# Delta-net chunk inversion by squaring 8x8 blocks on TensorE, decays loaded in rows, scalings on ScalarE

## The chip, the core and the metric

The kernel runs on one core of one Trainium2 chip. Five engines work side by side, each through its own queue in program order: TensorE (PE, matrix products into PSUM), VectorE (DVE), ScalarE (ACT), GpSimd (POOL) and SyncE (SP, which here only issues DMAs). The metric is the device time of one execution in microseconds (us), as the median of several runs.

## The reference

One layer of a hybrid model over 256 latent and 256 context tokens of width 2048: a modulated norm, one input projection, two token mixers side by side (RWKV-7 with 16 heads of 64, gated DeltaNet with 8 heads of 128, both in two directions), a gated merge, an output projection, then a SwiGLU feed-forward. The change touches the DeltaNet mixer:

```python
gc = jnp.cumsum(chunks(g), axis=-1)                      # 64 tokens in a chunk
diff = gc[..., :, None] - gc[..., None, :]
decay = jnp.where(incl, jnp.exp(jnp.where(incl, diff, 0.0)), 0.0)
kb = kc * bc[..., None]
lmat = jnp.where(strict, jnp.einsum('nbhik,nbhjk->nbhij', kb, kc) * decay, 0.0)
rhs = jnp.concatenate([vc * bc[..., None], kb * jnp.exp(gc)[..., None]], axis=-1)
sol = lax.linalg.triangular_solve(lmat, rhs, left_side=True, lower=True, unit_diagonal=True)
```

So for each head, direction and chunk a unit triangular 64x64 matrix has to be inverted, from `lmat`, and `lmat` needs the decays between any two tokens, exp of a difference of running sums.

## The kernel before

Everything is fp32. Large projections are split into a high and a low part (`whi`, `wlo`) and done as three fast matmuls for each 128x128 weight tile; small products are plain fp32 matmuls, which the trace shows as two instructions each (a row of order says x8 where the profile says x16).

The program has four stretches. First the norm, the modulation and some low-rank projections (lines 404 to 522). Then the two mixers, woven together (lines 707 to 1481): the RWKV pairs `prepare`, `grams`, `inverse`, `values`, `scan` for p in 0..7, and the DeltaNet heads `features`, `tokens`, `decays`, `head_grams`, `head_inverse`, `head_scan` for h in 0..7. Then the merge and output projection (1485 to 1538), then the feed-forward (1541 to 1602).

In the woven stretch the pieces are Python generators. `Weave` (line 169) runs them against a table of costs and emits, on each engine, whichever instruction could start first by that table, with ranks for ties. This fixes the order on PE, DVE, ACT and POOL; at run time each queue goes through it strictly in that order. Filler for PE is `products` (line 1041), the projections of all heads with the lowest rank: 48 matmuls for each gate column block (256 columns) or for q, and 48 of 512 columns for k and v. The tables `GATES_A` and `GATES_B` (line 28) say behind which RWKV pair or DeltaNet head a gate block may be emitted: of the DeltaNet ones, 2 behind the grams of head 5, 6 behind those of head 6 and 8 behind those of head 7. `ada_rest` (line 1423) runs beside the DeltaNet heads: 96 tiles of a modulation weight, each with one DMA from POOL's queue and two DVE instructions (`aw`).

`invert` (line 552) does both mixers' inverses. It writes the matrices to DRAM (`scr`), reads the 16x16 diagonal blocks back one to a partition (`arena<-scr`), inverts them by substitution in 30 small DVE instructions (lines 583 to 588), writes them to DRAM (`tscr`), and reads them back in matrix layout (`T<-tscr`, `Tx<-tscr`). Two rounds on PE then double the blocks to 32 and to 64 (`double` in the change; lines 613 to 657 here). `head_inverse` (1317) joins two 64-blocks to 128 and writes `TF`. `decays` (1259) makes the decay matrix `Ed` of a head: DVE multiplies a mask by the gates (`arena<-C,gtok`), PE sums it (`pa<-arena,C`, 512 columns), ACT takes exp, POOL masks; a second matmul of 256 columns gives the row factor for `Qe`. `tokens` (1234) scales the transposed keys into `keg` and `kta`; `head_scan` (1351) goes through the four chunks, with `Vn` scaled by the gate `btok`.

PSUM is handed out as banks: `pib` one bank (inverses), `pab` two (everything else of a head), `psb` two (scans), `mmb` three (projections).

Of the kernel before, what the change touches and what calls it, by code (L numbers as in the profile page):

```python
# [18 lines left out]
P = 128  # L19
# [35 lines left out]
def const_array():  # L55
    c = np.zeros((P, NC_COLS), np.float32)

    def put(name, a):
        lo, hi = _C[name]
        c[:, lo:hi] = np.asarray(a, np.float32).reshape(P, hi - lo)  # L60

    i = np.arange(P)
    put("ident", np.eye(P))
    put("ones", np.ones((P, P)))
    put("bd64", (i[:, None] // 64) == (i[None] // 64))
    s, t = (i % 64)[:, None], np.arange(64)[None]
# [4 lines left out]
    put("qmask", np.concatenate([(same & (rb % 2 == 1))[:, even], (same & (rb % 2 == 0))[:, ~even]], 1))  # L71
    u = i[:, None]
    v = i[None]
    put("tri", np.concatenate([u <= v, u >= v], 1))
    put("aft", np.concatenate([u > v, u < v], 1))
# [192 lines left out]
def emit(ctx: ExitStack, tc, A, out, dbg=None):  # L268
# [34 lines left out]
    qmask = c_("qmask").rearrange("p (d a c) -> p d a c", d=2, a=2)  # L303
    tri = c_("tri").rearrange("p (d t) -> p d t", d=2)
    aft = c_("aft").rearrange("p (d t) -> p d t", d=2)
# [23 lines left out]
    zero = cst.tile([P, 130], F32, name="zero")  # L329
    G.memset(zero, 0.0)  # L330
# [74 lines left out]
    with tc.tile_pool(name="p0", bufs=1) as p0, \  # L405
# [95 lines left out]
        for part in range(NE + 1):  # L501
            if part < NE:
                ps = pst(pmm, "mm")
            for c in range(4):
                if part + 1 < NE:
                    load_ada(part + 1, c)
                if part < NE:
                    ada_part(ps, part, c)
                if c == 0 and part < NE:
                    w = low_split(part)  # L510
                    if part + 1 < NE:
                        load_low(part + 1)
                for _ in itertools.islice(before or (), (0, 1, 2, 1)[c]):
                    pass
            if part < NE:
                rows_of(part, ps, before or ())
                before = low_products(part, w)
            else:
                for _ in before:
                    pass  # L520
        for t in tscr:
            Q.dma_start(t.rearrange("(p a n) -> p a n", p=P, a=8), zero.unsqueeze(1).to_broadcast([P, 8, 130]))
# [29 lines left out]
    def invert(pool, Lt, parts, nu, which, full, fill):  # L552

# [42 lines left out]
        yield v.transpose(T0[:, us[1]], Tx[:, us[1]])  # L596

# [6 lines left out]

        def half(t, d):
            ax = "p u"[:2 * len(t.shape) - 3]
            return t.rearrange(f"{ax} (a b c) -> {ax} a b c", a=2, b=2)[..., d, :]

        def mm(ps, d, lhs, rhs):
            return [e.matmul(ps[64 * h:64 * h + 64, 32 * i:32 * i + 32], lhs(h, h2 * d + i), rhs(h, h2 * d + i),  # L610
                             start=True, stop=True) for i in range(h2) for h in range(2)]

        Qm = xt[:, :32 * nu].rearrange("p (u c) -> p u c", c=32)
        for d in range(2):
            T0d = half(T0[:, us[d]], d)
            ps = yield pib
            yield mm(ps, d, Lt, lambda h, u: half(N_(h, u), d))
            pv = ps[:, 0:32 * h2].rearrange("p (i a c) -> p i a c", a=2, c=16)
            yield v.tensor_mul(Qm[:, us[d]].rearrange("p i (a c) -> p i a c", a=2), pv,
                               qmask[:, d].unsqueeze(1).to_broadcast([P, h2, 2, 16]))  # L620
            yield mm(ps, d, Nt_, lambda h, u: Qm[64 * h:64 * h + 64, u, :])
            yield v.tensor_add(T0d, pv, T0d)
            weave.release(pib)
            yield v.transpose(Tx[:, us[d]], T0[:, us[d]])
# [19 lines left out]
        qo = pool.tile([P, h2, 32], F32, tag="ivo", name="qo")  # L644
# [6 lines left out]
        if full:  # L651
# [3 lines left out]
            for h in range(2):  # L655
# [8 lines left out]
    abd = dpool.tile([4, 32, P], F32, name="abd")  # L664
    gtok = cst.tile([P, 4, 16], F32, name="gtok")
# [12 lines left out]
               ("ivo", 256, 1), ("iv0", 1024, 1), ("v", 512, 1), ("gt", T, 1))  # L678
# [362 lines left out]
    def products():  # L1041
# [24 lines left out]
        while todo or nxt:  # L1066
# [27 lines left out]
            else:  # L1094
# [5 lines left out]
    gplaces = (("kvq", 1280, 2), ("l2s", 512, 1), ("gm", 512, 1), ("Ed0", 512, 1), ("Ed1", 512, 1), ("eq", T, 1), ("ob", 8 * T, 1),  # L1100
               ("NW", 1024, 1), ("O", T, 1), ("gy2", T, 1), ("q3", T, 1), ("XT", 512, 1), ("prod", 64, 1))
    shared = dict(kta=("LAl0", 1024, 3), LTg=("LAl1", 1024, 3), keg=("ivx", 1024, 2), iv0=("LAc0", 512, 3), ivx=("LAc0", 512, 3),
                  vt=("LAc1", 512, 3), PT0=("LAc1", 512, 3), PT1=("Pm", 512, 3), Qe=("Pm", 512, 3), Vn=("bon", T, 3), ivo=("bon", T, 3),
# [24 lines left out]
    gs = Shared()  # L1128
    hd = [{} for _ in range(NGH)]
# [6 lines left out]
    def begin():  # L1136
# [6 lines left out]
        t2 = gs.tile([P, 512], F32, tag="gm", name="t2")[:, 0:P]  # L1143
# [12 lines left out]
        for n in (15, 13, 11, 9, 7, 5, 3):  # L1156
# [5 lines left out]
        yield v.tensor_scalar(sp, sp, al, -1.0, ALU.mult, ALU.mult)  # L1162
        ps = yield pab
        yield [e.transpose(ps[:, 0:P], sp, ident), e.transpose(ps[:, P:2 * P], bet, ident)]
# [4 lines left out]
        yield [e.matmul(ps[:, T + 64 * i + 32 * d:T + 64 * i + 32 * d + 32], m[:, d], gtok[:, :, 8 * d:8 * d + 8], start=True, stop=True)  # L1169
               for d in range(2) for i, m in enumerate((tri, aft))] + [e.matmul(ps[:, 3 * P:3 * P + 64], ones, gtok, start=True, stop=True)]  # L1170
        for i, t in enumerate((egc, eta)):
            for d in range(2):
                o = T + 64 * i + 32 * d
                yield s.activation(t[:, :, 8 * d:8 * d + 8], ps[:, o:o + 32].rearrange("p (b c) -> p b c", b=4), AF.Exp)
        yield s.activation(egl, ps[:, 3 * P:3 * P + 64].rearrange("p (b c) -> p b c", b=4), AF.Exp)
# [38 lines left out]
    def features(h):  # L1214
# [5 lines left out]
        if h > 1:  # L1220
            for n in ("tok", "gram"):
                yield n, h - 2
# [11 lines left out]
    def tokens(h):  # L1234
# [24 lines left out]
    def decays(h):  # L1259
# [3 lines left out]
        if h:  # L1263
            yield "gram", h - 1
        o["Ed"] = Ed = []
        qe = []
        for d in range(2):
            col = 8 * d + h
            gm = gs.tile([P, 4, P], F32, tag="gm", name="gm")
            yield v.tensor_mul(gm, tri[:, d].unsqueeze(1).to_broadcast([P, 4, P]),  # L1270
                               gtok[:, :, col:col + 1].to_broadcast([P, 4, P]))
            gf = gm.rearrange("p b c -> p (b c)")
# [4 lines left out]
            weave.release(pab)  # L1277
            yield g.tensor_mul(ed, ed, tri[:, d].unsqueeze(1).to_broadcast([P, 4, P]))
            Ed.append(ed)
            if d == 0:  # L1280
                yield "feat", h
                yield "scan", NPAIR - 1 if h else NPAIR - 2
                if h > 1:
                    yield "gscan", h - 2
                o["Qe"] = gs.tile([P, 2, T], F32, tag="Qe", name="Qe")
            ps = yield pab
            yield e.matmul(ps[:, :T], ones, gf[:, 0:T], start=True, stop=True)
            eq = gs.tile([P, T], F32, tag="eq", name="eq")
            yield s.activation(eq, ps[:, :T], AF.Exp)
            weave.release(pab)  # L1290
            yield v.tensor_mul(o["Qe"][:, d], o["q"], eq)
        weave.ready("decay", h)

    def head_grams(h):
        o = hd[h]
        yield "decay", h
        if h > 1:
            yield "gscan", h - 2
        k, q, Ed = o["k"], o["q"], o["Ed"]
        o["LT"] = LT = gs.tile([P, 8, P], F32, tag="LTg", name="LT")  # L1300
# [16 lines left out]
    def head_inverse(h):  # L1317
# [4 lines left out]
        else:  # L1322
# [4 lines left out]
                                           lambda hh, d: [(0, LT[64 * hh:64 * hh + 64, 4 * d:4 * d + 4, 64 * hh:64 * hh + 64])],  # L1327
                                           8, h % 2, True, v)
# [22 lines left out]
    def head_scan(h):  # L1351
# [3 lines left out]
        yield "tok", h  # L1355
        if h:
# [15 lines left out]
        for n in range(4):  # L1372
# [6 lines left out]
            for d in range(2):  # L1379
                yield v.tensor_scalar_mul(Vn[:, d, :], ps[:, P * d:P * d + P], btok[:, bs[d], 8 * d + h:8 * d + h + 1])  # L1380
# [318 lines left out]
```

## Time and profile before

| what | us |
|---|---|
| median of 3 runs (2339.14 to 2345.67) | 2342.38 |
| the profiled execution | 2348.77 |
| its span, first to last instruction | 2346.7 |
| outside the span | 2.1 |
| grams of DeltaNet head 0 to grams of head 7 (span time 836 to 1303) | 467 |
| from there to the end of the woven stretch (1303 to 1388) | 85 |

The span is followed on a clock that starts with the first instruction. RWKV pairs run from about 100 to 840, DeltaNet heads from about 800 to 1388, the rest of the layer from 1388 to 2347. A row of the profile names an instruction by line, engine and operation, then its output and inputs by the program's names. Since helpers record the woven instructions, they all carry line 142 (DMAs line 153), and are told apart by their names.

### The profile page before, as it was taken

Reading aid. Unit: us, or ns where it says so; the run is one execution under the profiler, and the core shown is the slowest. Engines: PE = TensorE matmul, PEld = TensorE weight load, DVE = VectorE, ACT = ScalarE, POOL = GpSimd, SP = SyncE. Lnnn points to the kernel's source line nnn. Section 1 sums busy time; section 2 is a strip of 40 time slices with the busy share of each in tenths; the row PEclk is TensorE's granted clock in tenths of the full one; section 3 lists DMA queues with packets and bytes.
Section 4 is the critical chain, followed back from the end, with each engine's and each line's share of the span. In section 5 each row is a group of like instructions: output and inputs, shape, how many; then the busy total and the mean of one; then the engine's idle time right before and its main releaser. Section 6 shows DMA issues by size and latency. Waiting matters only on the chain. (4 is left out here: it accounts for less than half of the span.)

```text
span 2346.7 us, 51488 instructions
## 1 busy us (share of the span) xinstructions
PE 2223.8 (95%) x21368; PEld 1951.7 (83%) x21368; DVE 1557.2 (66%) x3237; ACT 1047.9 (45%) x1863; POOL 113.5 (5%) x183
## 2 busy tenths in 40 slices
PE   7988999999999999999798999999999999999998
PEld 4767677778788777776677989999999999999997
DVE  3447588778986489889878645765666556545454
ACT  3246454544355544344234346544444444444443
POOL 0000000000000011111111003000000000000000
PEclk9999999999999999999789999999999999999999
DMA  9956454434344256657466565663777776566665
GB/s 377 397 148 189 152 134 102 111 83 117 100 109 133 85 172 207 189 167 217 145 191 194 182 219 180 209 214 107 239 233 234 234 238 218 187 185 194 191 191 165
DMA packets 232570, 430.58 MB, mean 183 GB/s; under 512 B 114832, under 2 KB 130064, under 8 KB 227984
## 3 DMA queue, kind: packets, MB, share of 16 engines
q1 hardware_dynamic: 204688, 351.78, 48.4%
q0 software_dynamic: 13824, 50.34, 7.0%
q10 hardware_dynamic: 13824, 25.17, 3.5%
q8 instruction: 167, 2.74, 0.5%
q14 instruction: 67, 0.55, 0.1%
HBM read 401.45 MB, written 25.77 MB: 182 GB/s over the span
## 5 line engine op out<-in xcount | busy, mean ns | idle before, releaser
L357 DVE TENSOR_TENSOR wlo<-wraw,whi 128x1024 fp32r<-128x1024 f32 x328 | 393.5, 1200 | 351.1 <-ACT whi L356 348.2
L356 ACT CAST whi<-wraw 128x1024 fp32r<-128x1024 f32 x328 | 337.7, 1030 | 472.8 <-PE mm L367 413.8
L142 PE MATMUL mm<-hxh,wlo 128*128 128x256 f32 (+1 forms) x1376 | 468.3, 340 | 9.9 <-DVE wlo L142 9.7
L142 PE MATMUL mm<-hxh,whi 128*128 128x256 f32 (+1 forms) x1376 | 469.0, 341 | 3.4 <-ACT whi L142 3.3
L142 PE MATMUL mm<-hxl,whi 128*128 128x256 f32 (+1 forms) x1376 | 468.3, 340 | 0.0
L368 PE MATMUL mm<-hfh,wlo 128*128 128x256 f32 x1344 | 377.1, 281 | 0.4 <-DVE wlo L357 0.4
L366 PE MATMUL mm<-hfh,whi 128*128 128x256 f32 x1344 | 376.5, 280 | 0.0
L367 PE MATMUL mm<-hfl,whi 128*128 128x256 f32 x1344 | 375.2, 279 | 0.0
L142 PEld LDWEIGHTS mm<-hxh,wlo 128*128 128x128 f32 x1376 | 265.6, 193 | 39.4 <-DVE wlo L142 13.0
L142 PEld LDWEIGHTS mm<-hxh,whi 128*128 128x128 f32 x1376 | 265.6, 193 | 31.5 <-issue 6.5
L142 PEld LDWEIGHTS mm<-hxl,whi 128*128 128x128 f32 x1376 | 265.8, 193 | 27.2 <-issue 6.1
L142 DVE TENSOR_TENSOR wlo<-wraw,whi 128x512 fp32r<-128x512 f32 x344 | 236.2, 690 | 62.7 <-ACT whi L142 60.0
L142 ACT CAST whi<-wraw 128x512 fp32r<-128x512 f32 x344 | 205.8, 618 | 112.1 <-PE mm L142 88.9
L366 PEld LDWEIGHTS mm<-hfh,whi 128*128 128x128 f32 x1344 | 253.4, 189 | 0.0
L368 PEld LDWEIGHTS mm<-hfh,wlo 128*128 128x128 f32 x1344 | 252.8, 188 | 0.6 <-DVE wlo L357 0.6
L367 PEld LDWEIGHTS mm<-hfl,whi 128*128 128x128 f32 x1344 | 253.2, 188 | 0.0
L142 DVE TENSOR_TENSOR arena<-arena 128x28 f32<-128x28 f32 (+13 forms) x538 | 132.0, 247 | 32.1 <-DMA arena<-scr 20.4
L366 PE MATMUL mm<-za,whi 128*128 128x256 f32 x512 | 141.8, 277 | 0.0
L367 PE MATMUL mm<-za,whi 128*128 128x256 f32 x512 | 141.7, 277 | 0.0
L368 PE MATMUL mm<-za,wlo 128*128 128x256 f32 x512 | 141.6, 277 | 0.0
L142 DVE SCALAR_TENSOR_TENSOR aw<-aw,ck 128x512 f32<-128x512 f32 x180 | 131.2, 739 | 5.1 <-DMA aw<-ada_rest 4.4
L368 PEld LDWEIGHTS mm<-za,wlo 128*128 128x128 f32 x512 | 96.2, 188 | 0.0
(311 smaller groups left out, 3924.5 us busy)
## 6 DMA issues: line engine op xcount, KB each, us to landing
wraw<-w SPq DMA_DIRECT2D x172, 512.0 KB, 4.3
wraw<-wgu SPq DMA_DIRECT2D x168, 512.0 KB, 4.5
aw<-ada_rest POOLq DMA_DIRECT2D x96, 512.0 KB, 4.7
aw<-ada_first SPq DMA_DIRECT2D x32, 1024.0 KB, 11.5
wraw<-wdn SPq DMA_DIRECT2D x64, 448.0 KB, 3.7
wraw<-wout SPq DMA_DIRECT2D x32, 512.0 KB, 4.7
aw<-ada_gt ACTq DMA_DIRECT2D x64, 256.0 KB, 5.0
wraw<-wdn SPq DMA_DIRECT2D x32, 512.0 KB, 3.6
```

Of the source, the lines that this page charges most:

```text
L142: return Op(self, cost, lambda: getattr(self.engine, name)(out, *a, **k), split)
L356: S.copy(hi[:, c, :M], raw[:, c, :M])
L357: V.tensor_sub(lo[:, c, :M], raw[:, c, :M], hi[:, c, :M].bitcast(F32))
L366: E.matmul(ps, hi, Xh[:, k, :n], start=first and i == 0, stop=False)
L367: E.matmul(ps, hi, Xl[:, k, :n], start=False, stop=False)
L368: E.matmul(ps, lo, Xh[:, k, :n], start=False, stop=last and i == len(wt) - 1)
```

## The change

The DeltaNet heads (`which` is None) no longer take the way through DRAM. `by_squares` cuts out the 8x8 diagonal blocks D with a mask, and forms (1+D)(1+D^2)(1+D^4), which is the inverse exactly since D^8 is zero, in five groups of 16 matmuls of 64x64. One more doubling step, from 8 to 16, follows, with the same code that doubles 16 to 32; that code now takes both directions in one bank instead of one after the other, for the RWKV pairs too. The decays are loaded: `begin` forms running sums of the gates once by two scans, stores them in DRAM (`cumd`), and each head loads its rows to all partitions with two DMAs. DVE then subtracts and clips at zero in eight instructions a head. `keg`, `kta` and `Vn` are scaled on ACT, in instructions of 128 columns. `Qe` becomes a step of its own that others wait for.

```diff
-                  ("qmask", 64), ("tri", 256), ("aft", 256), ("q4", 4), ("q2", 2),
+                  ("qmask", 64), ("m8", 128), ("qmask8", 64), ("tri", 256), ("q4", 4), ("q2", 2),
...
+    def by_squares(pool, Lt, parts, nu):
...
+        for h in range(2):
+            yield v.tensor_mul(*(t.rearrange("p (d u) c -> p d u c", d=2) for t in (a[hs[h]], parts(h))),
+                               m8[hs[h]].to_broadcast([64, 2, nu // 2, 64]))
+        yield v.transpose(b, a)
+        p1 = yield pib
+        p2 = yield pab
+        yield mm(p1, a, b) + mm(p2, b, a)
+        for h in range(2):
+            yield v.tensor_add(c[hs[h]], b[hs[h]], ident[hs[h], hs[h]].unsqueeze(1).to_broadcast([64, nu, 64]))
+        yield s.copy(flat(E2[:, 0]), p1)
+        weave.release(pib)
+        yield v.tensor_copy(flat(E2[:, 1]), p2)
+        weave.release(pab)
+        p1 = yield pib
+        p2 = yield pab
+        yield mm(p1, E2[:, 1], c) + mm(p2, E2[:, 0], E2[:, 1])
+        yield v.tensor_add(flat(b), p1, flat(c))
+        weave.release(pib)
+        yield s.copy(flat(a), p2)
+        weave.release(pab)
+        p1 = yield pib
+        yield mm(p1, a, b)
+        yield v.tensor_add(flat(c), p1, flat(b))
+        weave.release(pib)
+        yield v.transpose(b, c)
+        yield from double(8, Lt, c, b, flat(a), nu)
+        return c, b, flat(a)
+
+    def double(n, Lt, T0, Tx, xt, nu):
...
+        yield mm(ps, Lt, lambda h, u, d: half(T0[64 * h:64 * h + 64, u, :], d))
+        for d in range(2):
+            yield v.tensor_mul(Qm[:, us[d]].rearrange("p i (a c) -> p i a c", a=na), pv[:, us[d]],
+                               qmask[n == 8][:, d].unsqueeze(1).to_broadcast([P, h2, na, n]))
+        yield mm(ps, lambda h, u: Tx[64 * h:64 * h + 64, u, :], lambda h, u, d: Qm[64 * h:64 * h + 64, u, :])
...
+        T0, Tx, xt = yield from (by_rows(pool, parts, nu, which, fill) if which is not None else by_squares(pool, Lt, parts, nu))
...
     (tokens)
-            yield v.tensor_mul(keg[:, d], p4, egc[:, :, col:col + 1].to_broadcast([P, 4, P]))
-            yield v.tensor_mul(kta[:, d], p4, eta[:, :, col:col + 1].to_broadcast([P, 4, P]))
+            for b in range(4):
+                yield s.activation(keg[:, d, b], p4[:, b], AF.Identity, scale=egc[:, b, col:col + 1])
+                yield s.activation(kta[:, d, b], p4[:, b], AF.Identity, scale=eta[:, b, col:col + 1])
...
     (decays)
-            yield v.tensor_mul(gm, tri[:, d].unsqueeze(1).to_broadcast([P, 4, P]),
-                               gtok[:, :, col:col + 1].to_broadcast([P, 4, P]))
-            yield e.matmul(ps, aft[:, d], gf, start=True, stop=True)
-            yield s.activation(ed.rearrange("p b c -> p (b c)"), ps, AF.Exp)
+            yield dq(ed, bass.AP(a.tensor, a.offset + col * P, [[0, P], [32 * P, 4], [1, P]]))
+            yield s.activation(eq, ed[:, 0:2].rearrange("p b c -> p (b c)"), AF.Exp)
+            for b in range(4):
+                yield v.tensor_scalar(ed[:, b], ed[:, b], gtok[:, b, col:col + 1], 0.0, ALU.add, ALU.min)
+            yield s.activation(ed, ed, AF.Exp)
...
-            ps = yield pab
-            yield e.matmul(ps[:, :T], ones, gf[:, 0:T], start=True, stop=True)
...
     (head_scan)
-                yield v.tensor_scalar_mul(Vn[:, d, :], ps[:, P * d:P * d + P], btok[:, bs[d], 8 * d + h:8 * d + h + 1])
+                yield s.activation(Vn[:, d, :], ps[:, P * d:P * d + P], AF.Identity, scale=btok[:, bs[d], 8 * d + h:8 * d + h + 1])
```

Three places show how the order moves. On DVE, before, at the start of the substitution of head 6: `arena<-arena 64x...` are its steps, `Vn` and `St` belong to the scan of head 5, `aw` to the modulation rows, and `wlo` is the low part of a projection weight.

```order
L142 TENSOR_SCALAR Vn<-s,btok 128x128
L142 SCALAR_TENSOR_TENSOR aw<-aw,ck 128x512 x2
L142 TENSOR_TENSOR arena<-arena 64x15 x2
L142 COPY St<-s 128x128
L142 TENSOR_TENSOR arena<-arena 64x28
L142 COPY St<-s 128x128
L142 TENSOR_TENSOR arena<-arena 64x14x2
L142 TENSOR_TENSOR wlo<-wraw,whi 128x512
L142 TENSOR_TENSOR arena<-arena 64x39
```

On DVE in the change, inside `by_squares` of a head: `E` is the squared block copied from PSUM, `Dn` and `B` hold the growing product, `arena<-arena,gtok` are decay rows.

```order
L146 COPY E_9635<-pa 128x512
L146 SCALAR_TENSOR_TENSOR aw<-aw,ck 128x512 x2
L146 TENSOR_SCALAR arena<-arena,gtok 128x128 x4
L146 TENSOR_TENSOR Dn<-pi,B 128x512
L146 SCALAR_TENSOR_TENSOR St<-St,egl,s 128x128
L146 COPY arow<-pa 128x256
L146 SCALAR_TENSOR_TENSOR St<-St,egl,s 128x128
L146 TENSOR_TENSOR mod<-pa,PR 128x4 x2
L146 TENSOR_TENSOR wlo<-wraw,whi 128x512
L146 SCALAR_TENSOR_TENSOR arena<-mm,PR,arena 128x2x254
L146 TENSOR_TENSOR B<-pi,Dn 128x512
```

The 30 small steps between scan and weights have gone, a few steps of 512 columns stand in their place, and `Vn` is no longer in this queue.

On SP, before, the DMAs of head 6 from the gathered blocks on, among weight loads (`wraw`) and gate stores (`gts`):

```order
L153 DMA arena<-scr_105 64x16x16
L153 DMA wraw<-w 128x1024
L1019 DMA gts__1351<-arena 128x256
L153 DMA wraw<-w 128x1024 x3
L1019 DMA gts__1351<-arena 128x256
L153 DMA tscr_107<-arena 64x16x16
L153 DMA T_13699<-tscr_107 64x4x64
L153 DMA Tx<-tscr_107 64x4x64
L153 DMA T_13699<-tscr_107 64x4x64
L153 DMA Tx<-tscr_107 64x4x64
```

On SP in the change, two neighbouring heads:

```order
L157 DMA arena<-cumd_1337 128x4x128
L157 DMA arena<-cumd_1338 128x4x128
L157 DMA wraw<-w 128x1024 x8
L1083 DMA gts__1353<-arena 128x256
L157 DMA arena<-cumd_1337 128x4x128
L157 DMA arena<-cumd_1338 128x4x128
```

Ten DMAs of a head have become two, and these stand together.

On PE, before, in the doubling of head 6: `pi<-T,LT` and `pi<-arena,Tx` are 8 matmuls of one direction, `pa<-arena` the grams of head 7, `mm` a gate projection.

```order
L142 MATMUL pi<-T_13699,LT 64x32 x8
L142 MATMUL mm<-hxl,whi 128x256
L142 MATMUL pa<-arena 128x128 x4
L142 MATMUL mm<-hxh,wlo 128x256
L142 MATMUL pi<-arena,Tx 64x32 x8
L142 MATMUL mm<-hxh,whi 128x256
```

On PE in the change, inside `by_squares` of a head, beside the scan of the head before (`s`):

```order
L146 MATMUL s<-St,arena 128x128
L146 MATMUL pi<-B,E_9635 64x64 x16
L146 MATMUL pa<-E_9635 64x64 x16
L146 MATMUL s<-Vn,kta 128x128 x2
L146 MATMUL pa<-aw,C 32x256 x4
L146 MATMUL mm<-hxh,wlo 128x512
```

Groups of 16 matmuls that were not there before now stand in PE's queue, here directly ahead of a step of the scan. Counted over the whole order, PE has 80 matmuls of 64x64 and 32 of 64x32 more for each head, and two of 512 and two of 256 columns fewer. Projections of 256 columns (48 matmuls each) that stand behind the grams of head 7 are 11.7 in the change and 9.3 before; ahead of the grams of head 0 they are 28 and 29.

More of the change, by code (lines that the diff above doesn't have):

```diff
@@ L602, in Nt_ @@
             return Tx[64 * h:64 * h + 64, u, :]
[L605 to L624, printed above, removed]
+        yield from double(16, Lt, T0, Tx, xt, nu)
         quads = []
@@ L664, in emit @@
     abd = dpool.tile([4, 32, P], F32, name="abd")
+    cumd = [dpool.tile([P, P], F32, name=f"cumd{d}") for d in range(2)]
     gtok = cst.tile([P, 4, 16], F32, name="gtok")
@@ L1128, in emit @@
     gs = Shared()
+    lts = {}
     hd = [{} for _ in range(NGH)]
@@ L1264, in decays @@
             yield "gram", h - 1
+            yield "Qe", h - 1
         o["Ed"] = Ed = []
@@ L1296, in head_grams @@
         yield "decay", h
+        yield "feat", h
+        yield "scan", NPAIR - 1 if h else NPAIR - 2
         if h > 1:
@@ L1355, in head_scan @@
         yield "tok", h
+        yield "Qe", h
         if h:
```

117 lines of the change are left out of this document (79 added, 38 removed).

## The prediction

> **What bounds the kernel now.** I read the page first, then a table of busy times by stage.
>
> ```profile
> span 2346.7 us, 51488 instructions
> PE 2223.8 (95%) x21368; PEld 1951.7 (83%) x21368; DVE 1557.2 (66%) x3237; ACT 1047.9 (45%) x1863; POOL 113.5 (5%) x183
> ...
> core 0: us, PE busy (x) PEld busy (x) DVE busy (x) ACT busy (x) POOL busy (x), PEclk, DMA share, GB/s
> 300.00:750.00 450.00, 443.74 (x5711) 351.09 (x5709) 370.63 (x939) 218.56 (x542) 13.61 (x39) 0.99 0.42 111
> 836.00:1303.00 467.00, 418.19 (x3364) 343.35 (x3362) 396.13 (x979) 191.49 (x355) 70.44 (x110) 0.93 0.63 188
> 1303.00:1388.00 85.00, 79.87 (x927) 75.85 (x926) 48.95 (x133) 34.80 (x73) 0.00 (x0) 1.00 0.60 184
> 1388.00:2347.00 959.00, 931.14 (x7882) 925.53 (x7882) 536.85 (x716) 430.57 (x563) 21.23 (x16) 0.99 0.65 203
> ```
>
> The 95% of PE hides a difference. Among the RWKV pairs (300 to 750) PE is busy 443.7 of 450 us at a granted clock of 0.99: I call busy times clock over length the **yield** of PE, here 0.976. Between the grams of head 0 and of head 7 (836 to 1303) it is 418.2 x 0.93 / 467 = 0.833; behind them (to 1388) 79.9 x 1.00 / 85 = 0.94. Behind 1388 nothing is changed. So only the DeltaNet heads have room: 467 us with 49 us of PE idle and some 30 lost to the clock. DVE is busy 396 of the 467 us. What holds it up is seen in the waits of 836 to 1303, and what holds PE up beside it:
>
> ```profile
> DVE Tx L142 <- DMA T<-tscr: 20.2, 6, 5.9
> DVE arena L142 <- DMA arena<-scr: 17.1, 6, 7.1
> PE s L142 <- DVE St L142: 8.2, 2, 6.6
> PE pi L142 <- DMA T<-tscr: 7.4, 5, 3.3
> PE s L142 <- DVE Vn L142: 6.8, 9, 3.0
> ```
>
> DVE stands still 37.3 us for the inverses' way through DRAM. With its 396.1 busy that makes 433 of 467 us, 93%: in this stretch DVE, not PE, is the full engine, and PE waits for what stands late in DVE's queue (`St`, `Vn`). The timeline of the last head shows the chain itself.
>
> ```profile
> 1305.29 0.59 SPq L153 DMA_DIRECT2D scr<-LT  x1
> ...
> 1318.36 0.59 SPq L153 DMA_DIRECT2D arena<-scr  x1
> ...
> 1334.34 0.58 SPq L153 DMA_DIRECT2D tscr<-arena  x1
> ...
> 1339.42 0.60 SPq L153 DMA_DIRECT2D T<-tscr  x1
> ...
> 1343.61 0.66 PE L142 MATMUL pi<-T,LT 64*64 64x32 f32 x16
> ...
> 1365.67 0.37 ACT L142 COPY TF<-pi 64x256 f32<-64x256 f32 x1
> ```
>
> From the grams to `TF` it takes 60 us, 38 of them (1305.3 to 1343.6) before the first matmul. A head may take 467/7 = 66.7 us, so this serial chain fills most of a head.
>
> **The change, part by part.** First DVE, per head, from the groups of 836 to 1303 (seven heads); the last row, a wider transpose, is from the pairs' stretch.
>
> ```profile
> L142 DVE TENSOR_TENSOR arena<-arena 64x63 f32<-64x63 f32 x28 | 5.9, 209 | 0.3
> ...
> L142 DVE TENSOR_TENSOR arena<-arena 64x15 f32<-64x15 f32 x28 | 4.6, 165 | 17.5 <-DMA arena<-scr 17.1
> ...
> L142 DVE TENSOR_TENSOR keg<-pa,egc 128x512 f32<-128x512 f32 x14 | 9.5, 678 | 1.3 <-PE pa L142 1.3
> L142 DVE TENSOR_TENSOR arena<-C,gtok 128x512 f32<-128x512 f32 x14 | 9.4, 673 | 0.1
> L142 DVE TENSOR_SCALAR Vn<-s,btok 128x128 f32<-128x128 f32 x48 | 16.0, 336 | 1.6 <-PE s L142 1.6
> L142 DVE STREAM_TRANSPOSE Tx<-T 128x256 f32<-128x256 f32 x20 | 8.8, 438 | 20.2 <-DMA T<-tscr 20.2
> L142 DVE TENSOR_TENSOR arena<-pi,C 128x128 f32<-128x128 f32 x14 | 4.0, 286 | 2.0 <-PE pi L142 1.9
> L142 DVE TENSOR_TENSOR arena<-s,arena 128x128 f32<-128x128 f32 x12 | 3.0, 279 | 3.5 <-PE s L142 3.5
> L142 DVE STREAM_TRANSPOSE Tx<-arena 128x512 f32<-128x512 f32 x18 | 12.6, 703 | 1.2 <-DMA arena<-tscr 1.1
> ```
>
> It loses the 30 substitution steps (0.165 to 0.209 each; the eight groups are 40.3 us for seven heads, 5.8), four `keg`/`kta` scalings (2.7), two mask products (1.35), eight `Vn` (2.7), six transposes of 0.44 (2.6), two memsets (0.3): 15.4 us. It gains two cuts, two identity additions, two sums and one copy of 512 columns (7 x 0.68 = 4.7), four transposes of 0.70 (2.8), the masks and sums of one more doubling (4 x 0.28 = 1.1), and eight subtractions of 128 columns. These last are not in the trace in this form; the nearest row is 0.279, bounds are 0.165 (the smallest step) and 0.336: I take 0.28, 2.2 us. Sum 10.8, so DVE gets 4.6 us a head (4.1 to 5.5), some 32 us in the stretch, besides the 37.3 us of standing.
>
> Then PE, where the change costs. The rows show how long a group holds the queue until the next starts.
>
> ```profile
> 1291.58 1.02 PE L142 MATMUL pa<-arena,C 128*128 128x512 f32 x2
> 1292.04 0.68 PE L142 MATMUL mm<-hxh,wlo 128*128 128x256 f32 x1
> 1292.56 0.28 PE L142 MATMUL mm<-hxh,whi 128*128 128x256 f32 x1
> 1292.67 0.28 PE L142 MATMUL mm<-hxl,whi 128*128 128x256 f32 x1
> ...
> 1295.53 0.60 PE L142 MATMUL pa<-arena,C 128*128 128x256 f32 x2
> 1295.78 0.47 PE L142 MATMUL mm<-hxh,wlo 128*128 128x256 f32 x1
> ...
> 1296.29 0.66 PE L142 MATMUL pi<-T,LT 64*64 64x32 f32 x16
> 1296.88 0.40 PE L142 MATMUL mm<-hxl,whi 128*128 128x256 f32 x1
> ...
> 1312.44 0.68 PE L142 MATMUL pi<-T,LT 64*64 64x64 f32 x16
> ```
>
> A decay product holds PE 0.46 us, one of 256 columns 0.25, a projection matmul 0.115; 8 small matmuls of 32 columns 0.59, and of 64 columns by their 0.68 against 0.66 about 0.61. Five groups of 16 make at most 5 x 1.2 = 6.1 us. Part of the 0.6 is turning over between kinds, paid once in a joined group, so I take 5.3. One more doubling adds two groups of 16 (2.1); the old one, joined, saves 0.2; the decay products go (1.4). Net **5.8 us more a head** (5 to 7), 46 us for eight.
>
> ACT gets 16 scalings and 8 `Vn` of 128 columns and two copies of 512:
>
> ```profile
> L142 ACT COPY gvt<-pa 128x512 f32<-128x512 f32 x7 | 4.1, 585 | 2.4 <-PE pa L142 2.4
> ...
> L142 ACT COPY arena<-s 128x128 f32<-128x128 f32 x12 | 2.8, 264 | 15.3 <-PE s L142 15.3
> ...
> DMA to landing us min/median/max: 2.0/4.4/7.4
> ```
>
> 24 x 0.264 + 2 x 0.585 = 7.5 us a head; ACT was busy 191 of 467 us and comes to some 55%. I cost it at nothing: ACT's idle time covers it. Without that cover the casts behind it come late and PE pays up to those 7.5 us.
>
> On SP ten DMAs of a head become two, of 256 KB each. They wait for the decay tiles to be free of the head before, and the weight loads of the next projections are queued behind them; so were they behind the `scr` transfers. The landing row above is that of the `scr` transfers, 4.4 us in the middle. I cost the new loads at nothing, as they are issued most of a head's time ahead of the grams; uncovered it would be 4.4 us a head, and at best the shorter queue gains the same. For the RWKV pairs the joined doubling changes no amount of work, and PE is full there: nothing. The new sums in `begin` happen once.
>
> **The sum.** DVE's load falls to (396 - 32) = 364 us in the stretch and nothing stands for DRAM, so DVE no longer sets it; PE does. Work of PE at full clock from 836 to 1388 is now 418.2 x 0.93 + 79.9 = 469 us of 552. It becomes 469 + 46 + 5.5 = 520: the 5.5 (48 x 0.115) is one projection of 256 columns that stood ahead of head 0 and now stands behind; ahead of 836 the same 5.5 us is saved. The time is 520 over the yield PE then reaches. I take the middle of the two stretches where DVE is not the full engine, 0.976 among the pairs (with DVE at 82%) and 0.94 behind head 7: 0.958. That is 543 - 5.5 = 537 against 552: **-15 us**. The profiled execution took 2348.8 us, 6.4 above the median; taken from the median, 2327.
>
> By the Trainium skill (TensorE: Matmul & The Clock Gate, Part 1: The HAM clock gate) an idle window of about 3.4 us halves PE's clock and a busy one restores it. The trace agrees, 0.93 where PE idles 49 us and 0.99 where it idles 6, so by that rule closing gaps returns clock too, and the sum stays as it is, since the yield has it in.
>
> **Rivals.** (B) PE has far more room than its busy time says. For: in 836 to 1388 its weight loads (PEld) are busy only 419 of 552 us, 76%, but 925.5 of 959 behind. Then DVE alone sets the stretch: (396 - 32) / 0.93 = 391, 76 less; behind head 7, 2.4 more projections (13 us) and one inverse (5.8) stand, and 5.5 is saved ahead: -63, **2280**. The Trainium skill (Perfetto Trace Analysis, Identifying the Most-Contended Engine) says just this, that matmul busy time misleads and the share of weight loading is to be read. Against: among the pairs PE is 98% busy with PEld at 78%, and it never got denser in woven work.
>
> (C) The new groups stall PE. Each inverse gets seven more turns between PE and DVE or ACT, and a group that finds its operand late holds everything behind it in PE's queue, a step of the scan or a projection. For: PE already waits for `Vn` and `St`. Break-even is a yield of 520/557.5 = 0.933; the stretch as a whole has 0.85 now. At 0.90 it is 578 - 5.5 = 572: +20, **2362**.
>
> (D) The gain is given back behind head 7: `GATES_B` puts 14 gate blocks behind heads 6 and 7, PE is nearly full there, and 13 + 5.8 us are added. With 20 won ahead of it (head period 64 instead of 66.7) and 5.5 before, that leaves -6.7: **2336**.
>
> **Chances.** My forecast 0.48 (yield 0.945 to 0.976, -25 to -7), B 0.12, C 0.22, D 0.18. A difference within 0.3%, 7 us, could not be told from none. Faster by more: most of the forecast, B, and a third of D, 0.61; within: 0.17; slower: 0.22. The range takes in half of B below and half of C above, with the open DVE, PE and DMA costs inside: 2282 to 2362.
>
> **What would show it.** Right: no wait of DVE or PE for DRAM in the heads; DVE busy under 88% between the grams of heads 0 and 7, which come closer than 467 us; PE's yield above 0.94 and granted clock above 0.96 there; the stretch behind head 7 longer than 85 us. Wrong: `pi` groups of 64x64 waiting for DVE or ACT by more than 0.5 us each (C); PE busy in that stretch well under 0.9 and yet a shorter one (B); a group of 16 matmuls off 1.1 us; ACT above 65% with casts late.

## The result, and the profile after

The changed kernel takes 2366.95 us (median of 4 runs, 2363.01 to 2370.62), the kernel before 2340.98 in runs beside it: ratio 1.0108, 95% interval 1.0085 to 1.0131. It is slower by 26 us where 15 less were forecast, and lies above the range. Its profiled execution took 2363.0, the lowest of its four runs, and that of before 2348.8, above all of its timed runs; so the two traces show only 14 of the 26 us.

First the page, then the table of stages (its columns as in the prediction):

```profile
span 2361.2 us, 54836 instructions
PE 2245.5 (95%) x23090; PEld 1989.6 (84%) x23090; DVE 1537.4 (65%) x3001; ACT 1105.9 (47%) x2071; POOL 117.7 (5%) x183
```

```profile
818.00:1298.00 480.00, 437.25 (x5102) 369.02 (x5101) 384.99 (x802) 242.53 (x540) 75.63 (x112) 0.99 0.56 178
1298.00:1400.00 102.00, 93.60 (x1092) 91.06 (x1091) 48.82 (x94) 47.11 (x110) 0.00 (x0) 0.98 0.54 176
1400.00:2361.00 961.00, 939.62 (x7880) 935.01 (x7880) 535.87 (x714) 429.08 (x560) 21.90 (x16) 0.99 0.62 203
```

The grams of head 0 end at 818, 18 us earlier than before (5.5 were forecast), those of head 7 at 1298. The heads take 480 us for 467, the stretch behind them 102 for 85, the rest of the layer 961 for 959: -18 + 13 + 17 + 2 = +14. DVE has room (385 of 480 us, 80%) and PE's clock is at 0.99. Yet PE's yield in the heads is 437.25 x 0.99 / 480 = 0.902. From head 0's grams to the merge PE stood 54 us before (552 less 498 busy) and stands 51 now (582 less 531). The waits were exchanged for others. From the waits in the heads, the five largest of PE and one each of ACT and DVE (us in total, times, longest):

```profile
ACT arena L146 <- DMA arena<-cumd: 47.8, 7, 9.5
...
DVE arena L146 <- ACT arena L146: 31.9, 18, 5.9
...
PE s L146 <- ACT Vn L146: 15.1, 5, 5.2
...
PE s L146 <- DVE St L146: 6.8, 6, 3.2
...
PE pi L146 <- DVE Dn L146: 5.4, 5, 1.3
...
PE pa L146 <- ACT arena L146: 3.5, 6, 0.9
...
PE pi L146 <- DVE E L146: 3.2, 4, 1.5
```

No engine waits for `scr` or `tscr` in the heads any more, but ACT stands 47.8 us for the loaded decays. A stretch of the timeline, and the landing times of these loads:

```profile
1158.52 0.93 SPq L157 DMA_DIRECT2D arena<-cumd  x2
...
1169.17 0.42 ACT L146 ACTIVATE arena<-arena 128x256 f32<-128x256 f32 x1 [9.46 <-DMA arena<-cumd]
...
1170.00 0.62 ACT L146 ACTIVATE Vn<-s,btok 128x128 f32<-128x128 f32 x2
...
1170.41 1.01 PE L146 MATMUL s<-Vn,kta 128*128 128x128 f32 x3 [5.17 <-ACT Vn L146]
```

```profile
DMA to landing us min/median/max: 8.3/10.3/12.8
```

The loads go out right behind the grams of the head before, their first exponential is next in ACT's queue, `Vn` of the running scan stands behind it, and PE, in order too, behind `Vn`.

What ends the woven stretch is seen in both traces: the last projection on PE, the load of the merge's input, the merge's first product. Before:

```profile
1380.85 0.28 PE L142 MATMUL mm<-hxh,wlo 128*128 128x256 f32 x1
...
1381.16 0.38 SPq L1490 DMA_DIRECT2D PA<-oad  x1
...
1384.43 0.39 PE L142 MATMUL s<-PT,Vn 128*128 128x128 f32 x2
...
1388.59 0.79 PE L366 MATMUL mm<-oah,whi 128*128 128x256 f32 x2 [3.77 <-ACT oah L371]
```

After:

```profile
1391.32 0.28 PE L146 MATMUL mm<-hxh,wlo 128*128 128x256 f32 x1
...
1391.63 0.38 SPq L1566 DMA_DIRECT2D PA<-oad  x1
...
1400.12 0.58 PE L367 MATMUL mm<-oah,whi 128*128 128x256 f32 x1 [8.52 <-ACT oah L372]
```

In both the load leaves 0.31 us behind the last projection (the kernel puts `PA` where the projections' input lay), and the merge begins 7.4 and 8.5 us later. The last scan ends at 1385 before and, with the shorter inverses, at 1370 after; the projections, PE's filler, start their last product at 1381 and 1391. **Not the chain of inverses but the last projection on PE starts the merge, and it did so before the change as well**, which the prediction had missed.

Behind the merge the 959 and 961 us hide a difference. The down projection at the end of the layer is the same code in both kernels, and PE waits for nothing among these products, yet the same 512 of them are spread over 237.5 us before and 244.9 after:

```profile
L368 PE MATMUL mm<-za,wlo x512: 275/277/285, 2092.8 to 2330.3; 128*128 128x256 f32 x171
```

```profile
L369 PE MATMUL mm<-za,wlo x512: 277/280/285, 2100.2 to 2345.1; 128*128 128x256 f32 x171
```

It is 237.5 to 237.9 us in the traces of the kernel before and of its two variants below (`spare`, `ctl`), and 244.9 to 245.0 in those of the change and of all 16 kernels made from it. So **some 7 of the 26 us lie in code that the change leaves as it was.** Why is open: what all 17 share are other constants, other places of tiles in memory and the new order of waits, and no run alters one of these alone. The pair of traces hides it, since from the merge to the down projection the profiled execution of before took 704 us, `ctl` 693, `spare` 695 and the change 700.

### The profile page after: what moved, and what is told of

It reads as the page before. It is cut to its first block, busy times and chain, and to the rows that moved or that the text cites. A ratio compares the mean times of both kernels' runs of the same rounds, so it can differ in the third digit from the quotient of the medians.

```text
span 2361.2 us, 54836 instructions
## 1 busy us (share of the span) xinstructions
PE 2245.5 (95%) x23090; PEld 1989.6 (84%) x23090; DVE 1537.4 (65%) x3001; ACT 1105.9 (47%) x2071; POOL 117.7 (5%) x183
## 4 chain that ended last, share of the span: by engine, by line
PE 67%; DVE 13%; DMA 10%; issue 5%; ACT 4%; SPq 0%; POOL 0%; ACTq 0%; DVEq 0%; POOLq 0%
PE mm L146 16%; PE mm L367 12%; PE mm L369 12%; PE mm L368 12%; DVE arena L146 5%; PE s L146 5%; PE pa L146 3%; PE pi L146 3%; DMA arena<-cumd 2%; DVE wlo L146 2%; DVE aw L146 2%; DMA aw<-ada_rest 2%; DMA wr<-wgu 1%; PE mm L455 1%; ACT arena L146 1%
## 5 line engine op out<-in xcount | busy, mean ns | idle before, releaser
L358 DVE TENSOR_TENSOR wlo<-wraw,whi 128x1024 fp32r<-128x1024 f32 x328 | 393.2, 1199 | 365.0 <-ACT whi L357 358.7
L146 PE MATMUL mm<-hxh,whi 128*128 128x256 f32 (+1 forms) x1376 | 463.0, 336 | 3.2 <-ACT whi L146 3.2
L146 PE MATMUL mm<-hxl,whi 128*128 128x256 f32 (+1 forms) x1376 | 461.1, 335 | 0.0
L146 ACT ACTIVATE arena<-arena 128x512 f32<-128x512 f32 (+4 forms) x132 | 77.1, 593 | 121.3 <-DVE arena L146 54.3
```

The costliest lines, as they stand in the source:

```text
L146: return Op(self, cost, lambda: getattr(self.engine, name)(out, *a, **k), split)
L358: V.tensor_sub(lo[:, c, :M], raw[:, c, :M], hi[:, c, :M].bitcast(F32))
```

## The experiments

For each run PE's work (busy time x granted clock, added up over 10 us slices from 150 us to the first merge product) is set against that length; the rest, standing and lost clock, is called idle; it is read from one trace of each kernel. Before it is 1133 + 105 = 1238 us, after 1167 + 83 = 1250: +34 of work, -22 idle.

**Each part taken back alone.** Theory S: the loss is ACT's standing for the loads. W: it is PE's additional work. A: it is the scalings on ACT. `late8` alters the planner's idea of the load:

```diff
-            yield dq(ed, bass.AP(a.tensor, a.offset + col * P, [[0, P], [32 * P, 4], [1, P]]))
+            yield dq(ed, bass.AP(a.tensor, a.offset + col * P, [[0, P], [32 * P, 4], [1, P]])) + 8.0
```

> The changed kernel with one number altered: the planner is told that a decay row load takes 8 us more than it assumed, so that the first exponential stands later in ScalarE's queue; the work is the same. Theory S (ScalarE stands 47.8 us for these loads between the grams of head 0 and head 7, and Vn, needed by the scan, is queued behind): the waits of ScalarE for cumd fall under 10 us, those of PE for Vn from 15.1 to under 5, and the time falls by 12 to 25, to 2342 to 2355. Theory W (PE has too much more work, some 5.8 us a head, and its yield stays near 0.90 whatever the order): within 5 of 2367. Theory A (the 24 scalings a head on ScalarE are the trouble): within 5 of 2367.

In `no_load` the running sums and loads go and the two products a direction come back; in `no_act` these lines are exchanged; in `no_sq` `head_inverse` calls `by_rows`:

```diff
-                yield s.activation(keg[:, d, b], p4[:, b], AF.Identity, scale=egc[:, b, col:col + 1])
+            yield v.tensor_mul(keg[:, d], p4, egc[:, :, col:col + 1].to_broadcast([P, 4, P]))
...
-                                           lambda hh: LT[64 * hh:64 * hh + 64, :, 64 * hh:64 * hh + 64], 8, None, True, v)
+                                           lambda hh, d: [(0, LT[64 * hh:64 * hh + 64, 4 * d:4 * d + 4, 64 * hh:64 * hh + 64])], 8, h % 2, True, v)
```

> The changed kernel with the decays made by matmuls and exponentials from PSUM again, as before; squares and ScalarE scalings stay. PE gets 1.4 us a head more (11 us), DVE two mask products a head for eight subtractions. Theory S: the standing of ScalarE goes, worth 12 to 25, less up to 11 of PE work: 2345 to 2365. Theory W: 11 more, 2372 to 2380. Theory A: 2367 to 2378.

> The changed kernel with keg, kta and Vn scaled on VectorE again; squares and loaded decays stay. ScalarE loses some 9.3 us a head (16 x 0.40 and 8 x 0.365), VectorE gets 5.4 back. Theory A: ScalarE's queue runs free and the time falls by 10 or more, to 2357 or less. Theory S: Vn no longer stands behind the waiting exponential, so PE's 15.1 us of waits for Vn go too, 2350 to 2360, but ScalarE still stands some 48 us for the loads, and casts and NW stand behind it; this run tells A from W, not from S. Theory W: within 5 of 2367, or above by VectorE's work.

> The changed kernel with the substitution through DRAM again in the eight heads; loaded decays, ScalarE scalings and the joined doubling stay. Theory W: PE loses 7.4 us a head (59 in all), and the time falls to 2335 or less, below the kernel before. Theory S: the stall remains and the serial chain of 60 us a head is back beside it, VectorE has its 30 steps back: 2360 to 2385. Theory A: as S.

Measured: `late8` 2362.8 (ratio 1.0090, 1.0069 to 1.0111), `no_load` 2367.8 (1.0115, 1.0096 to 1.0135), `no_act` 2366.0 (1.0107, 1.0090 to 1.0124), `no_sq` 2370.5 (1.0125, 1.0091 to 1.0158). None gives the time back. In `late8` the waits for `Vn` and for `cumd` left the lists, and others came (PE's waits, then the heads' stage):

```profile
PE pi L146 <- DVE E L146: 7.3, 2, 5.3
PE pi L146 <- DVE Dn L146: 6.5, 5, 3.4
PE s L146 <- DVE St L146: 5.8, 9, 1.8
```

```profile
824.00:1298.00 474.00, 436.75 (x5068) 367.40 (x5067) 382.13 (x799) 241.08 (x535) 74.24 (x112) 0.98 0.58 180
```

Its yield, 436.75 x 0.98 / 474, is 0.903 as before. S falls as the main cause: the waits went as it said, the time did not. A falls with `no_act`. W was wrong on `no_sq`, which was to be 2335 or less, and on `no_load`, which was to be 2372 or more.

**Each part put in alone**, by the same edits in other combinations; `only_join` keeps of the change the joined doubling, the new order of waits and the places of tiles.

> The changed kernel with substitution, decays by matmul and VectorE scalings all back: what is left of the change is the joined doubling, in the pairs and the heads, and the order of waits that came with it. So far each of the three large parts taken out by itself left the time at 2363 to 2371. Theory J (what they share, the joined doubling, costs the 26 us): 2358 or more. Theory W (PE's additional work for the squares costs it, and what no_sq lost was ScalarE standing 58 us for the decay loads in a chain that is serial again): within 6 of 2340.

> Joined doubling and squares, with decays by matmul and VectorE scalings as before. Theory W: PE has 57 us more work than in the kernel before between the pairs and the merge (as in no_load, where 55 came out) and is the bound: 2360 to 2372. Theory J: 2358 or more also, and only_join tells them apart. Theory S2 (squares gain, and it is loads and scalings together that take it back): 2325 or less.

> Joined doubling and loaded decays, with substitution and VectorE scalings as before. Theory L (the loads make ScalarE stand some 50 us, and the inverse's serial chain with them; this is what no_sq lost): 2355 to 2372. Theory A (the ScalarE scalings are what no_sq lost): within 6 of only_join, or 5 below by 1.4 us of PE a head.

> Joined doubling and ScalarE scalings, with substitution and decays by matmul as before. Theory L: within 6 of only_join, or below it by up to 15, since VectorE, which has 433 of 467 us filled or standing in the kernel before, loses 5.4 us a head. Theory A: 2355 to 2372.

Measured, with work and idle of the traces (all but the first two rows have the joined doubling):

| kernel | us | ratio to before | work | idle |
|---|---|---|---|---|
| before | 2340 to 2344 | 1 | 1133 | 105 |
| `spare` (below) | 2374.9 | 1.0142 (1.0109 to 1.0175) | 1166 | 108 |
| `only_join` | 2354.1 | 1.0047 (1.0026 to 1.0068) | 1134 | 105 |
| `only_act` | 2356.6 | 1.0053 (1.0034 to 1.0072) | 1127 | 120 |
| `only_load` | 2368.1 | 1.0117 (1.0089 to 1.0146) | 1112 | 145 |
| `only_sq` | 2372.0 | 1.0124 (1.0098 to 1.0150) | 1189 | 72 |
| `no_sq` (load, act) | 2370.5 | 1.0125 (1.0091 to 1.0158) | 1109 | 139 |
| `no_load` (squares, act) | 2367.8 | 1.0115 (1.0096 to 1.0135) | 1187 | 70 |
| after (all three) | 2367.0 | 1.0108 (1.0085 to 1.0131) | 1167 | 83 |

`only_join` fell between its two theories. In the traces it begins the merge at 1389.2, where before did so at 1388.6 and `ctl` at 1392.2: nothing of its 11 us is lost ahead of the merge, and 7 of them are the slower down projection.

Squares add 56 us of PE work (`only_sq` to `only_join`) and take 33 of idle away: +18 in the medians. Loads take 22 of work away and, without squares, add 40 of idle: +14. With squares there, they take 20 and add 13, and nothing is left in the time. Where the idle of the loads is likely to come from is seen in the waits of `only_load`, in which the in-place subtractions of DVE stand behind the exponential on ACT:

```profile
ACT arena L146 <- DMA arena<-cumd: 45.5, 7, 9.0
...
DVE arena L146 <- ACT arena L146: 32.8, 10, 5.9
```

Scalings on ACT change nothing (2356.6 to 2354.1; `no_act` 2366.0 to 2367.0).

**What is PE's work worth, and what the chain?** `twice` issues four of the five square groups again, `detour` puts a round trip through DRAM into each inverse:

```diff
         yield mm(p1, a, b) + mm(p2, b, a)
+        yield mm(p1, a, b) + mm(p2, b, a)
...
         yield mm(p1, E2[:, 1], c) + mm(p2, E2[:, 0], E2[:, 1])
+        yield mm(p1, E2[:, 1], c) + mm(p2, E2[:, 0], E2[:, 1])
```

```diff
+    way = dpool.tile([P, 512], F32, name="way")
...
         yield v.transpose(b, c)
+        yield dq(way, flat(b))
+        yield dq(flat(b), way)
```

> The changed kernel with four of the five groups of 16 square products issued a second time, same operands and same result: some 4.2 us more of PE a head, 34 in all, and nothing else. Theory W (with squares PE is the bound; its work over a yield of 0.93 to 0.94): 36 more, 2395 to 2410. Theory F (the chain from features to grams sets the head period and PE has slack in the inverse): 2367 to 2378.

> The changed kernel with one round trip through DRAM put into each inverse behind the squares (the transposed sum is written out and read back): some 9 us more from grams to TF in each head, no work on any engine. Theory W: the inverse's length no longer matters, within 6 of 2367, the last head's 9 us included since gates fill PE behind it. Rival I (the inverse still binds): eight times 9 behind one another, 2410 or more.

`twice`: 2396.1 (1.0234, 1.0199 to 1.0269), 29 us more for 32 more of work in its trace (1199). `detour`: 2365.9 (1.0102, 1.0072 to 1.0131), nothing. In the changed kernel the inverse's length does not matter any more, and nine tenths of the added PE work are paid. Does that hold for the kernel before? `spare` repeats its token transposes, whose results stand ready 80 us or more ahead of their scan; `ctl` only shuffles the order.

```diff
-        yield [e.transpose(ps[:, P * b:P * b + P], o["v"][:, P * b:P * b + P], ident) for b in range(4)]
+        yield [e.transpose(ps[:, P * b:P * b + P], o["v"][:, P * b:P * b + P], ident) for _ in range(6) for b in range(4)]
...
-        yield [e.transpose(ps[:, P * b:P * b + P], o["k"][:, P * b:P * b + P], ident) for b in range(4)]
+        yield [e.transpose(ps[:, P * b:P * b + P], o["k"][:, P * b:P * b + P], ident) for _ in range(6) for b in range(4)]
```

```diff
-LAT = dict(dma=2.4, v=1.0, s=1.0, hop=0.5, own=0.13, grp=32, crank=-1, cg=4, turn=0.09)
+LAT = dict(dma=2.4, v=1.0, s=1.0, hop=0.52, own=0.13, grp=32, crank=-1, cg=4, turn=0.09)
```

> The kernel before with the eight token transposes of each head written six times instead of once: 40 transposes of 0.109 us, 4.4 us more of PE a head, 35 in all (as much as in twice), none of it on the inverse's chain. Theory P (in the kernel before the serial inverse sets the heads' time and PE has room): 2342 to 2356. Rival (PE is the bound there too, as twice showed it for the changed kernel): 2368 to 2380.

> The kernel before with one number of the planner changed (hop 0.50 to 0.52): the same instructions, dealt out in another order. Theory N (an order alone moves the time by some 10 us, and the 11 us of only_join are no more than that): off 2342 by 6 to 15, either way. Rival J (the joined doubling costs them): within 5 of 2342.

`spare` took 2374.9: 34 us more for 33 of work, in a kernel whose PE was thought to have room. Its stages (to the grams of head 0, to those of head 7, to the merge):

```profile
700.00:837.00 137.00, 136.75 (x1437) 107.45 (x1436) 79.27 (x197) 71.22 (x166) 4.65 (x6) 1.00 0.34 99
837.00:1327.00 490.00, 438.34 (x3642) 362.69 (x3642) 396.07 (x978) 186.40 (x347) 71.38 (x110) 0.94 0.58 176
1327.00:1424.00 97.00, 87.37 (x930) 84.15 (x928) 51.87 (x135) 40.51 (x85) 0.00 (x0) 0.97 0.59 183
```

PE stands 52 us in the 490 and stood 49 in the 467: the work lengthened the stretch and filled none of its gaps. (The transposes also hold one of the two `pab` banks longer; whether that costs anything was not tried.) Again the merge's load leaves 0.31 us behind the last projection (1415.61 and 1415.30). `ctl` took 2341.0 (0.9992, 0.9971 to 1.0013): this one shuffle moved nothing.

**Loads told later, without squares.**

> Joined doubling and loaded decays with substitution and VectorE scalings, the planner told 8 us more for a load (only_load was 2368 with the load's exponential early in ScalarE's queue and the in-place subtractions of VectorE behind it). Theory LS (in the serial chain it is this standing, of VectorE too, that lengthens a head from 65 to 71 us): the inverses come 65 to 67 us apart again, and with 22 us less PE work than only_join: 2335 to 2350. Rival Q (the loads hold up the chain's own transfers through DRAM): 2360 or more.

> As the run before, with ScalarE scalings too, which take 5.4 us a head from VectorE. Theory LS: as the run before or up to 10 below, 2330 to 2350. Rival Q: 2360 or more.

`no_sq_late8` took 2354.4 (1.0048, 1.0031 to 1.0064), 16 less than `no_sq`; `load_late8` 2368.2 (1.0113, 1.0074 to 1.0153), the same as `only_load`. Neither run came into the range of LS. With scalings on ACT, emitting the loads' exponentials later is worth those 16 us. With scalings on DVE the trace of `load_late8` does begin the merge 18 us earlier than that of `only_load` (1389 for 1407), but its last scan ends only at 1432, beside the merge, and from the merge on it takes 12 us longer (969 for 957); why is not settled.

**Mixtures and the doubling.** `mix3` and `mix4a` choose by head; `pairs_split` and `split_late8` bring the old doubling back, in two halves, for the pairs or everywhere.

```diff
-                                           lambda hh: LT[64 * hh:64 * hh + 64, :, 64 * hh:64 * hh + 64], 8, None, True, v)
+                                           (lambda hh: LT[64 * hh:64 * hh + 64, :, 64 * hh:64 * hh + 64]) if h in SQ else
+                                           lambda hh, d: [(0, LT[64 * hh:64 * hh + 64, 4 * d:4 * d + 4, 64 * hh:64 * hh + 64])],
+                                           8, None if h in SQ else h % 2, True, v)
```

> Joined doubling, decays by matmul, VectorE scalings; heads 1, 3 and 5 inverted by squares, the other five by substitution. If the two bounds change over as the runs say (PE work over 0.94 with squares, the serial chain of 65 us a head with substitution), three heads of squares add 21 us of PE work and take some 10 us each out of the chain: 2325 to 2342. Rival (both kinds of head stall PE in their own way): 2350 to 2365.

> As the run before with heads 0, 2, 4 and 6 by squares, and keg, kta and Vn on ScalarE, which takes 5.4 us a head from VectorE, by whose queue the substitution's steps go. By the two bounds: 28 us more of PE work, 40 out of the chain: 2325 to 2345. Rival: 2350 to 2365.

> The changed kernel with the doubling of the RWKV pairs' inverses in two halves again, as before; the heads' inverses stay as changed. If the 11 us that only_join lost are the joined doubling among the pairs, where PE is full: 2352 to 2360. If they belong to the heads or to the waits that came with it: within 5 of 2367.

> The run no_sq_late8 (substitution, ScalarE scalings, loaded decays with 8 us more in the planner; 2354) with all doublings in two halves again: the change without squares and without joining, and the loads told later. If joining costs 11 us wherever it stands: 2338 to 2347, with 22 us less PE work than the kernel before perhaps under it. If not: within 5 of 2354.

`mix3` 2370.5 (1.0126, 1.0092 to 1.0160; work 1157, idle 97), `mix4a` 2363.8 (1.0100, 1.0065 to 1.0135; 1157, 95): my picture of two bounds that change over head by head was wrong (`mix3` lies above both of its ranges), and no mixture gains. `pairs_split` 2364.6 (1.0110, 1.0093 to 1.0128) and `split_late8` 2357.6 (1.0077, 1.0054 to 1.0101): the joined doubling isn't what `only_join` lost. Both still have the slower down projection. What is left of the change in `only_join`, the waits for `Qe`, `feat` and `scan`, the constants and the places of tiles, wasn't tried apart. No version came out under the kernel before.

## Why the prediction was wrong

**The step that failed** is the yield: "DVE no longer sets it, PE does", and PE then reaches 0.958. Work was forecast well, 520 us from head 0's grams to the merge, and 437.25 x 0.99 + 93.6 x 0.98 = 525 came. Idle was to be 543 - 520 = 23 us there; it is 582 - 525 = 57, a yield of 0.902. The first half of the sentence came true (DVE at 80%, no DRAM wait in the inverses), the conclusion did not: PE's 54 us of standing stayed at 51 when DVE had room. In their place stand back-and-forth waits of a few tenths to 5 us that each new order deals out anew. And the yield was taken from stretches that hold little such traffic.

Part of the missing yield belongs to the loads. `no_load`, with squares but without them, has in its trace, from head 0's grams to those of head 7 and on to the merge:

```profile
841.00:1314.00 473.00, 448.91 (x5083) 375.35 (x5082) 380.38 (x749) 240.97 (x537) 73.20 (x111) 0.99 0.54 173
1314.00:1407.00 93.00, 85.67 (x1024) 83.09 (x1022) 45.38 (x87) 39.88 (x87) 0.00 (x0) 0.98 0.54 180
```

PE stands 31 of these 566 us, and the yield is 0.934, the break-even of rival C. So even without the loads the squares brought nothing: `no_load` took 2367.8. That it was the shorter inverse which took standing away, and not room on DVE, is suggested by `only_act`: it takes 30 us from DVE over the program (1527 for 1557), and from 150 us to the merge PE stands 85 us there for 79 in `only_join`.

The step beneath it: the kernel before was read as held by a serial chain of 60 us a head, so PE's additional work was to run in free time. `spare` shows that work put elsewhere in PE's queue does not (34 us for 33). The merge waits for PE's last projection in both kernels, so the end moves with PE's whole work plus its standing. The squares' 56 us cost only 18 because they took 33 of idle along. Why `spare`'s work fills no gap is argued, not shown: each queue goes strictly in order, so work placed elsewhere in PE's queue is no help to an instruction that waits at its head.

**"Behind 1388 nothing is changed"** put at nothing what came to 7 us, in the down projection, for a reason that stays open.

**PE +46 us**: 34 came. The squares and the doubling were right, 56 for 57.6 (7.2 x 8). The decay products were undersized: 22 us in all, 2.7 a head and not 1.4. The row shown had it: behind such a product the first projection starts at 1292.04 and the next at 1292.56, 0.52 us on instead of 0.115; this turning back, 0.4 us there and by the 22 us some 0.3 after each of four products, was not counted.

**DVE -4.6 a head**: over the whole program 1557.2 became 1537.4, -2.5 a head. One row is larger than the 0.68 taken, the sum with the identity, two of 0.806, which explains 0.25 of the 2.1. Some rows that the change leaves alone are 2 to 3% longer too (`aw<-aw,ck` 0.756 for 0.739 us, `LT` 0.351 for 0.340); the rest is open. That row, and two of ACT:

```profile
L146 DVE TENSOR_TENSOR B<-Dn,C 64x512 f32<-64x512 f32 x14 | 11.3, 806 | 0.2
...
L146 ACT ACTIVATE keg<-pa,egc 128x128 f32<-128x128 f32 x54 | 21.4, 397 | 1.6 <-PE pa L146 1.6
L146 ACT ACTIVATE Vn<-s,btok 128x128 f32<-128x128 f32 x52 | 17.2, 365 | 25.8 <-PE s L146 25.8
```

**ACT +7.5 a head at nothing**: 1047.9 became 1105.9, 7.3 a head, and it cost nothing (`no_act`, `only_act`). The size is right partly by luck: one scaling takes 0.397 or 0.365, not the 0.264 of a copy, and 24 of them with two copies of 0.58 would be 10.4; but behind one another they overlap (two `Vn` in 0.62 us at 1170.00 above). The Trainium skill (ScalarE: Activation LUTs, What ACT_TABLE_LOAD costs) adds some 93 ns for each operand that is a column of values, to 186 ns + 0.833 ns an element. By that a scaling of 128 columns is estimated at 0.386 us; the rows are within 6% of it.

**The loads at nothing** was wrong in its cover: that they leave most of a head's time ahead of the grams is true, but it is ACT that stands for them, with the scan's `Vn` behind. They landed in 10.3 us, not 4.4. The saving of 20 us of PE work brought nothing (`no_load` 2367.8 to 2367.0). That the standing ate it is argued: in `late8`, where ACT no longer waits for the loads, idle is still 79 us, for 70 without loads.

**Rivals.** C gave 2362 and a yield of 0.90, and 2367 and 0.902 came. Its sign came too: the `pi` groups that waited did so for 1.1 us (`Dn`) and 0.8 (`E`) each. But its place was only in part right, since the groups of the inverse account for some 11 us of PE's waits, and when the largest wait, `Vn`, went (`late8`), the yield stayed. That its time came so close is partly luck, as C knew nothing of the 7 us behind the merge or of the loads. D's place was right, more projections behind head 7 (102 us for 85), without the gain ahead of it. B was wrong: PE's weight loads at 76% were no room. Of the signs named beforehand, DVE under 88%, the clock above 0.96, ACT near 55% (242.5 of 480, 51%), a stretch of 102 us behind head 7 and about 1 us for a group of 16 (`twice`: 32 groups, 32 us) came; heads closer than 467 us and a yield above 0.94 did not.

## What to carry to other kernels

Ask what starts the next stage, and read it at the stage's end: here the merge's load left 0.31 us behind PE's last filler, so work added to PE was paid nearly in full (`twice`, `spare`), however much PE stood on the way. Standing of an in-order engine is room only if an experiment has put work into it; a few dozen repeated instructions in the old kernel (`spare`) would have told it. Compare the stretches that nobody changed, too, and in more than one trace: 7 of the 26 us were there. And when a computed value becomes a loaded one, look at who stands in the consumer's queue behind the wait, not only at when the value is needed.

## What the runs showed of the hardware

After the 5.2 us of standing at 1165 in the changed kernel the granted clock was 0.83 over the next ten:

```profile
1165.00:1170.00 5.00, 0.24 (x10) 0.10 (x4) 0.39 (x2) 0.83 (x3) 0.00 (x0) 1.00 0.74 219
1170.00:1180.00 10.00, 8.49 (x90) 7.07 (x91) 9.93 (x21) 3.24 (x10) 2.20 (x1) 0.83 0.24 83
```

The change's 22 us less of idle are clock won back, not standing. From 150 us to the merge PE stood 73 us before (1238 less 1165 busy) and 73 after (1250 less 1177); lost clock fell from 32 us (1165 - 1133) to 9 (1177 - 1167). Its parts differ: the squares alone (`only_sq` to `only_join`) took 24 us of standing and 9 of lost clock away, the loads alone (`only_load` to `only_join`) added 25 and 15, and beside the squares (`no_load` to the change) 18 of standing and no lost clock. How much clock goes with a given standing differs from trace to trace: `detour` stood 70 us and lost 22 where the change stood 73 and lost 9, and no run shows why.
